# Splitting 512-column products into two of 256, and moving two early transfers, in a two-layer transformer trunk

## The chip, the cores and the metric

The kernel runs on one core of one Trainium2 chip. The metric is the device time of one execution in microseconds (us). The time of the kernel before is the median of three runs. One more execution was profiled, and all rows below come from that one.

## The reference

The reference computes a small decoder trunk on `x` of 256 tokens by 1024 features, all in float32. Layer 0 is differential attention (8 heads, each the difference of two softmaxes over causal scores with a relative-position bias, then an RMS norm per head), a residual with layer norm, and a squared-ReLU MLP of width 4096 with residual and layer norm. Layer 1 has the same shape, with plain 16-head causal attention over a shared K/V in place of the differential one (at 256 tokens there is one block, so the block selection selects nothing).

```python
for layer in range(DEPTH):                       # DEPTH = 2
    mix = diff_attention(h, ...) if layer == 0 else moba_attention(h, ...)
    h = layer_norm(ALPHA * h + mix, ln1_g[layer], ln1_b[layer])
    h = layer_norm(ALPHA * h + square(relu(h @ w_up[layer])) @ w_down[layer],
                   ln2_g[layer], ln2_b[layer])
```

## The kernel before

Every large product is done to nearly float32 precision as three products of operands that are cut in two: a high part and the rest, "hi" and "lo". `three` (L136 to L147) issues hi·hi, hi·lo and lo·hi into one PSUM accumulation. It has two forms. With `moving_w` (L141 to L143) the activations are the stationary operand, 128 tokens wide, and the weights stream past, 512 columns at a time: V, the output projection (`mix`), the first quarter of the MLP's upward product (`up_rows`) and all of its downward product (`down`) are done so. Otherwise (L145 to L147) the weights are stationary and 256 tokens stream past: the Q/K projections (`project`) and the rest of the upward product (`up`). Each product is one weight load and one matmul on TensorE.

All weights stream from memory in units of 128x2048 float32, each in two pieces of 128x1024. `fetch` (L86 to L90) issues the transfer of a piece into one of five `raw` buffers, on SyncE's queue. ScalarE copies the piece to `whi` (L103), VectorE subtracts to get `wlo` (L115), and then the next piece is fetched into the buffer that came free. `bg(n, True)` does `n` such pieces at the place in the program order where it stands; the engines work in that order.

The first two units are special. Eight "chunks" of 128x768 hold, for one block of 128 features each, the transposed input and the first 512 columns of V's weights. `fetch_chunk` puts chunks 0 and 1 into `xres` and chunks 2 to 6 into the five `raw` buffers; chunk 7 is fetched in `v_first`, when chunk 2 has been split (`kk == 2`). When chunks 3 to 7 have been split, `v_first` fetches pieces 4 to 8 (`fetch(kk + 1)`), the first pieces of the units that follow. `V` is a tile of 128x2x1024 that first gets a value after `v_first`, by `v_out`.

Near the end of layer 0's attention the program order is: V's last unit (`v_unit(u0 + 11, 1, 1)`), the exponentials of the last head (`softmax_a(7)`), two pieces, the normalization of that head (`softmax_b(7)`), V's copy out of PSUM (`v_out`), the scaling of the first four heads (`scale`), the transposes of the last head (`turn(7)`) and their copy (`turned(7)`), the transposes of the scaled heads (`o_turn`), and the products with V (`values`). `turn` and `o_turn` take turns in two PSUM banks.

The MLP runs `up` and `down` alternately, so its stages are about 11 us of 256-column products and 11 us of 512-column products in turn. The very last columns of the kernel (the second half of the columns of the second 128 tokens) are already done as products of 256 columns with moving weights.

Of the kernel before, what the change touches and what calls it, by code (L numbers as in the profile page):

```python
# [30 lines left out]
S = 256  # L31
DEPTH = 2
NK = D // P
# [19 lines left out]
def trunk(ctx: ExitStack, tc: tile.TileContext, x, first, units, lam_a, subln, rel_bias,  # L53
          ln_g, ln_b, ident_in, out):
    nc = tc.nc
# [29 lines left out]
    def fetch(q):  # L85

        if q < NU * PER:
            v, s = divmod(q, PER)
            raws[q] = wpool.tile([P, PIECE], F32, name="raw", bufs=RAWS)
            nc.sync.dma_start(raws[q], units[v, s])  # L90
# [30 lines left out]
    def bg(most=8, force=False):  # L121

        while most > 0 and (force or state["credit"] >= 1.0 / PER):
            if not piece():
                state["credit"] = min(state["credit"], 1.0)
                return
            state["credit"] -= 1.0 / PER
            most -= 1
# [8 lines left out]
    def three(ps, w, a, moving_w, n, start, stop):  # L137

        state["credit"] += n * PACE
        if moving_w:  # L140
            nc.tensor.matmul(ps, a[0], w[0], start=start, stop=False)  # L141
            nc.tensor.matmul(ps, a[0], w[1], start=False, stop=False)  # L142
            nc.tensor.matmul(ps, a[1], w[0], start=False, stop=stop)  # L143
        else:
            nc.tensor.matmul(ps, w[0], a[0], start=start, stop=False)  # L145
            nc.tensor.matmul(ps, w[0], a[1], start=False, stop=False)  # L146
            nc.tensor.matmul(ps, w[1], a[0], start=False, stop=stop)  # L147
# [7 lines left out]
    def at(k, h):  # L155
        return act[0][:, k, tokens(h)], act[1][:, k, tokens(h)]

    xres = const.tile([P, 2, D], F32, name="xres")
    chunks = {}

    def fetch_chunk(k):

        if k < 2:
            chunks[k] = xres[:, k, :S + 512]
        else:
            chunks[k] = wpool.tile([P, PIECE], F32, name="raw", bufs=RAWS)[:, :S + 512]
        if k == 0:
            nc.sync.dma_start(chunks[k][:, :S], first[k][:, :S])
            nc.scalar.dma_start(chunks[k][:, S:], first[k][:, S:])
        else:  # L170
            nc.sync.dma_start(chunks[k], first[k])
# [164 lines left out]
    def attention(layer, u0):  # L336
# [4 lines left out]
        with tc.tile_pool(name=f"attn{layer}", bufs=2) as pool, \  # L341
                tc.tile_pool(name=f"attnc{layer}", bufs=1) as one:
            V = one.tile([P, 2, D], F32, name="V")
# [17 lines left out]
            def v_first(u):  # L361

                if u == 0:
                    for h in range(2):
                        pv[0, h] = bank("a")
                split[u] = (wpool.tile([P, 2048], F32R, name="whi", bufs=AHEAD),
                            wpool.tile([P, 2048], F32R, name="wlo", bufs=AHEAD))
                hi, lo = (w.rearrange("p (k c) -> p k c", k=4) for w in split[u])
                for k in range(4):
                    kk = 4 * u + k  # L370
                    split_to(act[0][:, kk], act[1][:, kk], chunks[kk][:, :S])
                    split_to(hi[:, k], lo[:, k], chunks[kk][:, S:])
                    if kk == 2:
                        fetch_chunk(7)
                    elif kk > 2:
                        fetch(kk + 1)
                    if kk == 6:
                        nc.scalar.dma_start(scr, line)
                    a = [at(kk, h) for h in range(2)]
                    for h in range(2):  # L380
                        nc.tensor.matmul(pv[0, h], a[h][0], hi[:, k], start=kk == 0, stop=False)
                    for h in range(2):
                        nc.tensor.matmul(pv[0, h], a[h][1], hi[:, k], start=False, stop=False)
                    for h in range(2):
                        nc.tensor.matmul(pv[0, h], a[h][0], lo[:, k], start=False, stop=kk == NK - 1)
                state["piece"] = state["head"] = (u + 1) * PER
                state["credit"] += PACE
                used.add(u)

            if layer == 0:  # L390
                v_first(0)
                v_first(1)
                free.update(used)
                bg()
                for h in range(2):
                    v_out(0, h)
            else:
                for h in range(2):
                    for c in range(2):
                        pv[c, h] = bank("a")  # L400
                        for g in range(2):
                            u = u0 + 2 * c + g
                            hi, lo = unit(u, k=4)
                            for k in range(4):
                                three(pv[c, h], (hi[:, k], lo[:, k]), at(4 * g + k, h), True, 1 / 8,
                                      g == 0 and k == 0, g == 1 and k == 3)
                                if (h, c, g) == (0, 1, 1) and k % 2 == 0:
                                    ln_turn(1, k // 2)
                            if h == 1:
                                used.add(u)  # L410
                                bg(2, True)
                        v_out(c, h)
# [94 lines left out]
            def turn(p):  # L507
                t, _ = T.pop(p)
                AT[p] = []
                for m in range(1 if diff else 2):  # L510
                    pt = bank("c")
                    for j in range(3):
                        k = (j + 2) % 3
                        nc.tensor.transpose(pt[:, j * P:(j + 1) * P], t[:, m, k * P:(k + 1) * P], ident)  # L514
                    AT[p].append(pt)
# [124 lines left out]
            if diff:  # L640
                turn(5)
                v_unit(u0 + 10, 1, 0)
                halves_hi(7)
                softmax_a(6)
                halves_lo(7)
                turned(5)
                scale = rms(0, [O[0][:, h] for h in range(2)], nc.gpsimd)
                bg(1)
                softmax_b(6)
                scores(7)  # L650
                turn(6)
                v_unit(u0 + 11, 1, 1)
                turned(6)
                softmax_a(7)
                bg(2, True)
                softmax_b(7)
                for h in range(2):
                    v_out(1, h)
                for h in range(2):
                    scale(h)  # L660
                turn(7)
                turned(7)
                o_turn(0, 0)
                o_turn(0, 1)
                bg(2, True)
                for p in range(4, 8):
                    values(p)
                mix(0, 0, G0)
                scale = rms(4, po, nc.vector)
                scale(0)  # L670
                scale(1)
                bg(3, True)
                mix(0, 1, G0)
                mix(1, 0, G0[:2])
                o_turn(4, 0)
                mix(1, 0, G0[2:])
                o_turn(4, 1)
                bg(2, True)
                for c in range(2):
                    mix(0, c, G1)  # L680
                    if c == 0:
                        bg(1, True)
                    ln_add(0, c * 512, c * 512 + 512, pw[0, c])
                ln_apply(layer, 0, 512)
                bg(1, True)
                mix(1, 1, G0)
            else:
                turn(5)
                mix(0, 0, G0[:2])
                values(4)  # L690
                turned(5)
                mix(0, 0, G0[2:])
                halves_hi(7)
                softmax_a(6)
                halves_lo(7)
                softmax_b(6)
                scores(7)
                values(5)
                turn(6)
                mix(0, 1, G0)  # L700
                softmax_a(7)
                turned(6)
                collect(4)
                bg(1, True)
                softmax_b(7)
                bg(1, True)
                values(6)
                mix(1, 0, G0)
                turn(7)
                turned(7)  # L710
                bg(2, True)
                mix(0, 0, G1[:2])
                values(7)
                collect(6)
                mix(0, 1, G1[:2])
                bg(1, True)
                for c in range(2):
                    mix(0, c, G1[2:])
                    ln_add(0, c * 512, c * 512 + 512, pw[0, c])
                ln_apply(layer, 0, 512)  # L720
                mix(1, 1, G0)
# [257 lines left out]
```

## Time and profile before

| | |
|---|---|
| median of 3 runs | 594.53 us (593.96 to 594.57) |
| profiled execution: time | 595.0 us |
| profiled execution: span | 592.9 us |
| TensorE matmuls: busy | 580.7 us, 98% of the span, 3768 matmuls |
| TensorE weight loads: busy | 515.6 us, 87% |
| VectorE, ScalarE busy | 377.7 us (64%), 318.8 us (54%) |
| mean granted TensorE clock | 0.996 of full speed |

The span is what the profiler saw of the engines; the 2.1 us between it and the execution's time lie around it. Matmuls overlap in the profile, since each one's duration runs to the end of its pipeline; what a product costs in a dense stretch is therefore the distance from its start to the next one's start.

### The profile page before, as it was taken

Reading aid. Unit: us, or ns where it says so; the run is one execution under the profiler, and the core shown is the slowest. Engines: PE = TensorE matmul, PEld = TensorE weight load, DVE = VectorE, ACT = ScalarE, POOL = GpSimd, SP = SyncE. Lnnn points to the kernel's source line nnn. Section 1 sums busy time; section 2 is a strip of 40 time slices with the busy share of each in tenths; the row PEclk is TensorE's granted clock in tenths of the full one; section 3 lists DMA queues with packets and bytes.
Section 4 is the critical chain, followed back from the end, with each engine's and each line's share of the span. In section 5 each row is a group of like instructions: output and inputs, shape, how many; then the busy total and the mean of one; then the engine's idle time right before and its main releaser. Section 6 shows DMA issues by size and latency. Waiting matters only on the chain.

```text
span 592.9 us, 9651 instructions
## 1 busy us (share of the span) xinstructions
PE 580.7 (98%) x3768; PEld 515.6 (87%) x3768; DVE 377.7 (64%) x692; ACT 318.8 (54%) x540; POOL 14.2 (2%) x45
## 2 busy tenths in 40 slices
PE   9999999999999999999999999999999999999993
PEld 7899978889899899898889999878899899899883
DVE  5787778976743734553877777697785544554236
ACT  5776787357664654552446556542785564564100
POOL 3000030000000000000000000000000000000000
PEclk9999999999999999999999999999999999999998
DMA  8996755547755737755249745151788556553002
GB/s 274 326 349 212 244 175 170 176 137 271 253 202 213 252 138 249 238 162 205 73 170 331 269 144 166 57 178 36 232 317 294 185 180 213 186 170 107 1 0 71
DMA packets 35548, 113.03 MB, mean 191 GB/s; under 512 B 3872, under 2 KB 8880, under 8 KB 35504
## 3 DMA queue, kind: packets, MB, share of 16 engines
q1 hardware_dynamic: 34144, 107.95, 53.2%
q0 software_dynamic: 1152, 4.19, 2.2%
q8 instruction: 29, 0.48, 0.3%
q10 hardware_dynamic: 208, 0.29, 0.1%
q14 instruction: 15, 0.12, 0.1%
HBM read 111.35 MB, written 1.07 MB: 190 GB/s over the span
## 4 chain that ended last, share of the span: by engine, by line
PE 93%; ACT 2%; DMA 2%; DVE 2%; issue 0%; SPq 0%; DVEq 0%; ACTq 0%
PE ps_b L145 12%; PE ps_b L147 12%; PE ps_b L146 12%; PE ps_a L143 12%; PE ps_a L142 12%; PE ps_a L141 12%; PE ps_b L141 4%; PE ps_b L143 4%; PE ps_b L142 4%; PE ps_a L461 2%; PE ps_c L290 1%; PE ps_c L514 1%; DMA raw<-in_first 1%; DMA raw<-in_units 1%; ACT whi L103 1%; PE ps_a L549 1%
## 5 line engine op out<-in xcount | busy, mean ns | idle before, releaser
L115 DVE TENSOR_TENSOR wlo<-raw,whi 128x1024 fp32r<-128x1024 f32 x188 | 222.2, 1220 | 57.8 <-ACT whi L103 55.8
L103 ACT ACTIVATE whi<-raw 128x1024 fp32r<-128x1024 f32 x188 | 190.1, 1052 | 71.9 <-PE ps_a L143 52.2
L145 PE MATMUL ps_b<-act_hi,whi 128*128 128x256 f32 x640 | 180.0, 281 | 0.0
L147 PE MATMUL ps_b<-act_hi,wlo 128*128 128x256 f32 x640 | 177.8, 278 | 0.8 <-DVE wlo L115 0.8
L146 PE MATMUL ps_b<-act_lo,whi 128*128 128x256 f32 x640 | 177.6, 278 | 0.0
L145 PEld LDWEIGHTS ps_b<-act_hi,whi 128*128 128x128 f32 x640 | 120.2, 188 | 1.7 <-issue 0.7
L147 PEld LDWEIGHTS ps_b<-act_hi,wlo 128*128 128x128 f32 x640 | 120.3, 188 | 1.1 <-DVE wlo L115 1.1
L146 PEld LDWEIGHTS ps_b<-act_lo,whi 128*128 128x128 f32 x640 | 120.7, 189 | 0.5
L143 PE MATMUL ps_a<-whi,h_lo 128*128 128x512 f32 x248 | 97.7, 394 | 0.0
L142 PE MATMUL ps_a<-wlo,h_hi 128*128 128x512 f32 x248 | 97.2, 392 | 0.0
L141 PE MATMUL ps_a<-whi,h_hi 128*128 128x512 f32 x248 | 96.5, 389 | 0.0
L74 DVE TENSOR_TENSOR h_lo<-sqr,h_hi 128x512 fp32r<-128x512 f32 x24 | 16.6, 692 | 77.6 <-ACT h_hi L72 77.6
L142 PEld LDWEIGHTS ps_a<-wlo,h_hi 128*128 128x128 f32 x248 | 46.6, 188 | 10.3
L141 PEld LDWEIGHTS ps_a<-whi,h_hi 128*128 128x128 f32 x248 | 46.6, 188 | 9.9
L143 PEld LDWEIGHTS ps_a<-whi,h_lo 128*128 128x128 f32 x248 | 46.6, 188 | 9.3
L751 ACT ACTIVATE relu<-ps_b 128x512 f32<-128x512 f32 x32 | 19.1, 596 | 65.4 <-PE ps_b L147 54.0
L481 ACT ACTIVATE t<-t,mx 128x256 f32<-128x256 f32 x64 | 28.4, 444 | 31.8 <-DVE mx L478 31.8
L141 PE MATMUL ps_b<-whi,act_hi 128*128 128x512 f32 x96 | 39.1, 407 | 0.0
L143 PE MATMUL ps_b<-whi,act_lo 128*128 128x512 f32 x96 | 37.7, 393 | 0.0
L142 PE MATMUL ps_b<-wlo,act_hi 128*128 128x512 f32 x96 | 37.5, 390 | 0.0
L141 PE MATMUL ps_a<-whi,act_hi 128*128 128x512 f32 x80 | 32.2, 402 | 0.0
L142 PE MATMUL ps_a<-wlo,act_hi 128*128 128x512 f32 x80 | 31.4, 392 | 0.0
(136 smaller groups left out, 587.1 us busy)
## 6 DMA issues: line engine op xcount, KB each, us to landing
raw<-in_units SPq DMA_DIRECT2D x188, 512.0 KB, 4.6
bias<-scr SPq DMA_DIRECT2D x16, 256.0 KB, 5.0
raw<-in_first SPq DMA_DIRECT2D x6, 384.0 KB, 6.1
lnp<-in_ln_g POOLq DMA_DIRECT2D x4, 512.0 KB, 4.3
lnp<-in_ln_b POOLq DMA_DIRECT2D x4, 512.0 KB, 5.4
xres<-in_x SPq DMA_DIRECT2D x1, 1024.0 KB, 5.6
out<-xres SPq DMA_DIRECT2D x2, 256.0 KB, 2.0
out<-xres SPq DMA_DIRECT2D x4, 128.0 KB, 1.9
```

The lines of the kernel that those rows point to most:

```text
L74: nc.vector.tensor_tensor(lo, src, hi.bitcast(F32), op=ALU.subtract)
L103: nc.scalar.activation(split[v][0][:, c], raws[state["head"]], AF.Copy)
L115: nc.vector.tensor_tensor(split[v][1][:, c], raws.pop(state["piece"]), split[v][0][:, c].bitcast(F32), op=ALU.subtract)
L141: nc.tensor.matmul(ps, a[0], w[0], start=start, stop=False)
L142: nc.tensor.matmul(ps, a[0], w[1], start=False, stop=False)
L143: nc.tensor.matmul(ps, a[1], w[0], start=False, stop=stop)
L145: nc.tensor.matmul(ps, w[0], a[0], start=start, stop=False)
L146: nc.tensor.matmul(ps, w[0], a[1], start=False, stop=False)
L147: nc.tensor.matmul(ps, w[1], a[0], start=False, stop=stop)
L461: nc.tensor.matmul(sc[m][:, c:c + n], a[r, q], b[r, :n], start=i == 0, stop=i == 2)
L481: nc.scalar.activation(t[:, m, s], t[:, m, s], AF.Exp, bias=mx[:, m, j:j + 1], accum_out=sm[:, m, j:j + 1])
L751: nc.scalar.activation(r, ps, AF.Relu)
```

## The change

A product of `three` with moving weights is no longer one matmul of 512 columns but two of 256 columns, one after the other, with the same stationary operand; each of the two has a weight load of its own. The first product of an accumulation (the one that opens it) stays whole. Chunk 7 goes into `V`'s own tile; its transfer is issued before `v_first` and not inside it, and the transfers of pieces 4 to 8 are each issued one chunk earlier. Near the end of layer 0's attention one of the two pieces moves from before `softmax_b(7)` to after `scale`, ahead of `turn(7)`.

```diff
         if moving_w:
-            nc.tensor.matmul(ps, a[0], w[0], start=start, stop=False)
-            nc.tensor.matmul(ps, a[0], w[1], start=False, stop=False)
-            nc.tensor.matmul(ps, a[1], w[0], start=False, stop=stop)
+
+            for i, (x, y) in enumerate(((0, 0), (0, 1), (1, 0))):
+                opens = start and i == 0
+                n = ps.shape[-1] if opens else 256
+                for c in range(0, ps.shape[-1], n):
+                    nc.tensor.matmul(ps[:, c:c + n], a[x], w[y][:, c:c + n],
+                                     start=opens, stop=stop and i == 2 and c + n == ps.shape[-1])
...
-    def fetch_chunk(k):
-
-        if k < 2:
+    def fetch_chunk(k, into=None):
+
+        if into is not None:
+            chunks[k] = into
+        elif k < 2:
             chunks[k] = xres[:, k, :S + 512]
...
-                    if kk == 2:
-                        fetch_chunk(7)
-                    elif kk > 2:
-                        fetch(kk + 1)
+                    if 2 <= kk < NK - 1:
+                        fetch(kk + 2)
...
             if layer == 0:
+                fetch_chunk(7, V[:, 0, :S + 512])
                 v_first(0)
                 v_first(1)
...
                 softmax_a(7)
-                bg(2, True)
+                bg(1, True)
                 softmax_b(7)
                 for h in range(2):
                     v_out(1, h)
                 for h in range(2):
                     scale(h)
+                bg(1, True)
                 turn(7)
                 turned(7)
```

## Rows read from the trace of the kernel before

**Rows 1.** The page: busy time by engine, and the chain that ended last.

```profile
PE 580.7 (98%) x3768; PEld 515.6 (87%) x3768; DVE 377.7 (64%) x692; ACT 318.8 (54%) x540; POOL 14.2 (2%) x45
PE 93%; ACT 2%; DMA 2%; DVE 2%; issue 0%; SPq 0%; DVEq 0%; ACTq 0%
```

**Rows 2.** The page's costliest groups: busy us, mean ns of one.

```profile
L146 PE MATMUL ps_b<-act_lo,whi 128*128 128x256 f32 x640 | 177.6, 278 | 0.0
...
L141 PE MATMUL ps_a<-whi,h_hi 128*128 128x512 f32 x248 | 96.5, 389 | 0.0
...
L141 PE MATMUL ps_b<-whi,act_hi 128*128 128x512 f32 x96 | 39.1, 407 | 0.0
...
L141 PE MATMUL ps_a<-whi,act_hi 128*128 128x512 f32 x80 | 32.2, 402 | 0.0
```

**Rows 3.** Timeline of TensorE, a run of 512-column products: start us, us.

```profile
267.21 0.39 PE L141 MATMUL ps_a<-whi,h_hi 128*128 128x512 f32 x1
...
276.82 0.39 PE L141 MATMUL ps_a<-whi,h_hi 128*128 128x512 f32 x1
```

**Rows 4.** Timeline of TensorE, the kernel's last columns, 256 at a time.

```profile
578.63 0.28 PE L141 MATMUL ps_b<-whi,h_hi 128*128 128x256 f32 x1
...
583.39 0.28 PE L141 MATMUL ps_b<-whi,h_hi 128*128 128x256 f32 x1
```

**Rows 5.** Timeline of TensorE, the first `up` stage of layer 0.

```profile
140.15 0.28 PE L145 MATMUL ps_b<-act_hi,whi 128*128 128x256 f32 x1
...
145.45 0.28 PE L145 MATMUL ps_b<-act_hi,whi 128*128 128x256 f32 x1
```

**Rows 6.** One line (L145), stretch 163.2 to 173 us: duration ns min/median/max.

```profile
L145 PE MATMUL ps_b<-act_hi,whi x29: 276/276/276, 163.3 to 172.8; 128*128 128x256 f32 x29
```

**Rows 7.** The same, 318 to 329 us (layer 1's first projections).

```profile
L145 PE MATMUL ps_b<-act_hi,whi x32: 281/281/281, 317.8 to 328.7; 128*128 128x256 f32 x32
```

**Rows 8.** Timeline of the start, all engines: start us, us, idle before and releaser.

```profile
13.32 0.42 ACT L72 ACTIVATE act_hi<-raw 128x256 fp32r<-128x256 f32 x1 [1.47 <-DMA raw<-in_first]
...
15.17 1.06 ACT L103 ACTIVATE whi<-raw 128x1024 fp32r<-128x1024 f32 x1 [0.92 <-DMA raw<-in_units]
...
16.26 1.22 DVE L115 TENSOR_TENSOR wlo<-raw,whi 128x1024 fp32r<-128x1024 f32 x1 [1.28 <-ACT whi L103]
...
16.51 0.28 PE L146 MATMUL ps_b<-act_lo,whi 128*128 128x256 f32 x1
...
17.54 0.39 PE L147 MATMUL ps_b<-act_hi,wlo 128*128 128x256 f32 x1 [0.75 <-DVE wlo L115]
```

**Rows 9.** SyncE's issues of line L171, all: duration ns, first and last start.

```profile
L171 SPq DMA_DIRECT2D raw<-in_first x6: 328/428/442, 1.6 to 8.6; - x6
```

**Rows 10.** Stretches of 1 us: busy by engine, granted clock, DMA share, GB/s.

```profile
10.00:11.00 1.00, 1.00 (x6) 0.80 (x5) 1.00 (x4) 0.98 (x3) 0.00 (x0) 1.00 0.67 218
...
13.00:14.00 1.00, 1.00 (x6) 0.79 (x6) 0.23 (x1) 0.68 (x2) 0.00 (x0) 1.00 0.70 164
```

**Rows 11.** Timeline around the last head of layer 0, all engines.

```profile
83.72 1.99 ACT L103 ACTIVATE whi<-raw 128x1024 fp32r<-128x1024 f32 x2
...
84.79 1.22 DVE L115 TENSOR_TENSOR wlo<-raw,whi 128x1024 fp32r<-128x1024 f32 x1 [1.75 <-ACT whi L103]
...
85.81 1.29 ACT L347 ACTIVATE V<-ps_a 128x512 f32<-128x512 f32 x2
...
86.06 0.40 PE L143 MATMUL ps_a<-whi,act_lo 128*128 128x512 f32 x1
...
87.32 0.52 PE L514 MATMUL ps_c<-ident,t 128*128 128x128 f32 x3 [0.86 <-DVE R L498]
87.87 0.49 ACT L523 ACTIVATE aT<-ps_c 128x384 f32<-128x384 f32 x1 [0.78 <-PE ps_c L514]
87.99 1.23 PE L290 MATMUL ps_c<-ident,o 128*128 128x128 f32 x8 [0.15 <-DVE o L580]
...
89.06 0.39 PE L538 MATMUL ps_a<-V,aT 128*128 128x128 f32 x2
```

## The prediction

> **What bounds the kernel now.** I read the page first: busy shares and the chain that ended last. TensorE's matmuls are busy 98% of the span, and 93% of the chain lies on TensorE [rows 1]; VectorE (64%) and ScalarE (54%) are far from it. So two things count: what TensorE pays for one product in a dense run, and the few places where it stands still. The page's groups give the number of products of each form [rows 2], but not their price: a matmul of 512 columns "lasts" 389 to 407 ns and one of 256 lasts 278, far more than the distance between two starts, because they overlap. The price comes from the timeline, by dividing a long gapless run by its count. The standing still comes from the timeline at the start and around layer 0's last head, which parts 2 and 3 read.
>
> **The price of a product.** In a run of 512-column products, 42 of them (14 triples) take 276.82 - 267.21 = 9.61 us, 228.8 ns each [rows 3]. The kernel's last columns are already done in the form that the change brings to all: moving weights, 256 columns, a weight load for each. There 42 products take 583.39 - 578.63 = 4.76 us, 113.3 ns each [rows 4]; a pair costs 226.7 ns, 2.1 less than one whole product. But 256-column products have a second pace. In the first `up` stage 45 of them take 145.45 - 140.15 = 5.30 us, 117.8 ns each [rows 5]; a pair would cost 235.6, 6.8 more than a whole one. The recorded duration tells the two paces apart: 276 ns where it is quick [rows 4, 6] and 281 where it is slow [rows 7]. Minimum, median and maximum agree over a whole stage (276/276/276 and 281/281/281), so it is not noise around one value: a run falls into one pace and stays there. What decides which I can't read from the trace. The stage of [rows 6] follows 512-column products and is quick; that of [rows 7] follows 512-column products too, and is slow; that of [rows 5] follows transposes. The group of [rows 2] with 256 columns (640 products, 177.6 us, so 277.5 ns each) says how often: (277.5 - 276) / (281 - 276) = 0.3, so some three in ten of today's 256-column products run slow, or a little fewer, since the first of a run is longer in any case.
>
> **Part 1, the split.** Moving weights of 512 columns are used in 248 + 96 + 80 = 424 triples [rows 2], 1,272 products. One opens each accumulation and stays whole: 6 for V, 8 for `mix`, 8 for `up_rows`, 8 for `down`, 30 in all. So 1,242 products become 2,484, with as many loads. All quick: 1,242 x -2.1 ns = -2.6 us. All slow: 1,242 x +6.8 ns = +8.4 us. These are the two ends. I take 95% quick: the only rows that show this very form are quick without exception, and they stand right behind 512-column products, as the split runs of V, `mix`, `up_rows` and the first `down` will stand behind the whole products that open them. That is 1,242 x (0.95 x -2.1 + 0.05 x 6.8) = -2.1 us. It lies on the path, as TensorE is the path, and nothing else changes pace: the credit that `three` gives to the background pieces is counted as before, and VectorE and ScalarE have a third of their time free [rows 1]. That more instructions must be issued costs nothing that I can find: a stage of 256-column products issues at this rate for 10 us without a gap [rows 6].
>
> **A rule against it.** The pair of [rows 4] shows no fixed price for a matmul beside its columns. The Trainium skill, "TensorE: Matmul & The Clock Gate", section "Back-to-back issue gap", gives the gap at full clock as the columns over 2.4 plus 2.5 ns; by that, 1,242 extra matmuls would cost 3.1 us and the sum would end slower. The quick rows disagree with it, the slow ones point its way.
>
> **Part 2, chunk 7 and the first pieces.** TensorE starts layer 0's first projection and stands still for the low part of piece 4: L146 starts at 16.51, L147 at 17.54 [rows 8]. Less one pace of 0.11, 0.92 us are lost. The chain back is short: `wlo` starts at 16.26, as soon as `whi` (15.17) is done, and `whi` waited 0.92 us for the transfer. That piece is asked for only when chunk 3 has been split, and chunk 7, six issues down the line, only at 8.6 us [rows 9], when chunk 2 has been split. The transfers then run dry: the DMA engines' share falls to 0.67 at 10 to 11 us and to 0.70 at 13 to 14 us [rows 10]. With chunk 7 asked for behind chunk 6, without a wait, and each piece one chunk earlier, these holes fill. One chunk is some 1.1 us of VectorE work or more (four subtractions and copies a chunk, VectorE busy all of 10 to 11 us [rows 10]), so piece 4 should land near 14.1, `whi` end at 15.2 and `wlo` at 16.4, just before 16.51. ScalarE is free then: chunk 7, which it took at 13.32 after 1.47 us of waiting [rows 8], comes earlier as well. From there TensorE is dense, so the gain lasts to the end. Bounds: -0.92 (the whole stall) and 0 (the transfers are bound by their rate, and the order alone changes). I take -0.9, since the two holes add up to 0.6 us of all DMA engines and the requests come a whole chunk earlier. `V` is not written until `v_out`, long after chunk 7 has been split, so its loan costs nothing.
>
> **Part 3, the moved piece.** TensorE's last V product starts at 86.06, and `turn(7)` only at 87.32, 0.86 us idle; then the first four transposes of `o_turn` at 87.99, and `values` at 89.06 [rows 11]. VectorE is late because of `wlo` at 84.79 (1.22 us), which waited for its `whi` [rows 11]. With that piece behind `scale`, `softmax_b` can start when the exponentials end near 83.8, and `turn(7)` follows V's products at once. But on ScalarE the second of the two `whi` (1.0 us of the 1.99) now stands between V's copies and `turned(7)`. The copies end at 85.81 + 1.29 = 87.10; `whi` then ends at 88.1, and the copy `aT` runs from 88.1 to 88.6 instead of from 87.87 to 88.36. The second half of `o_turn` needs the bank that `aT` reads, and then takes four transposes of 0.11: `values` start near 89.1, where they start now. TensorE's wait moves from ahead of `turn(7)` to the middle of `o_turn`. I take 0. Bounds: -0.9 if ScalarE doesn't hold it (`turn(7)`, `aT` and `o_turn` all move up by the idle time), +0.3 if `aT` is late by the whole 0.23 and the moved `wlo` then delays `act_lo`.
>
> **Sum.** -2.1 - 0.9 + 0 = -3.0 us. The profiled execution took 595.0, 0.5 above the median of 594.53; taken from the median, the forecast is 591.5.
>
> **Rivals.** *The two paces share as today.* At 0.3 slow, a product changes by 0.7 x -2.1 + 0.3 x 6.8 = +0.6 ns, together +0.7 us; with the start, -0.2: 594.3. For it: the entries into runs keep their kinds. Against it: whole-product runs, which now lie between stages, are gone. *A long stretch falls into the slow pace.* In each layer's MLP, `up` and `down` alternate for over 100 us with nothing between that could change the pace. In one layer 380 split products lose 6.8 + 2.1 ns (3.4 us), and 480 products of `up` that are quick today lose 4.5 ns each (2.2 us): -3.0 + 5.6 = +2.6, so 597.1; with both layers 602.7. It decides the sign when more than 0.32 of the split products are slow (8.9 ns x 0.32 - 2.1 = 0.72 ns, which is the 0.9 us of the start). For it: [rows 5, 7] are slow from end to end. Against: [rows 4]. *Every matmul has a fixed price.* If what [rows 5] show holds for any split (6.8 ns a pair), +8.4 - 0.9 = +7.5: 602.0. The Trainium skill's section named above is this rival's rule, with a smaller figure. *The start doesn't gain*, because the transfers are rate-bound: -2.1, so 592.4.
>
> **Chances and range.** Forecast 0.52; paces as today 0.20; a long slow stretch 0.17; a fixed price 0.05; no gain at the start 0.06. A difference of 0.2%, 1.2 us, is about what can be told from none. Faster than that: the forecast and the start's rival but for their near edge, and a fifth of the "as today" case: 0.60. Same: 0.14, most of the "as today" case. Slower: 0.26. The likeliest case's own range is 590.6 (-0.92 - 2.6 and a little from part 3) to 593.0 (no gain from one of the two terms). For 8 in 10 it must reach up to the case of one slow layer: 590.5 to 597.3.
>
> **What would show it.** Matmuls near 5,010. L141 to L143's successors with 256 columns at 276 ns, two starts 113.3 apart, in most stretches; 281 in a long one would prove the slow rival. No wait of TensorE for `wlo` at 16 to 18 us, chunk 7 copied before 13 us. Around the last head, `turn(7)` right behind V's products, `values` about as long behind V's last product as now (3.0 us). I am wrong if the 256-column stages that aren't touched change their pace, or if the load of a second equal weight costs or saves something that the last columns don't show.

## The result and the profile after

The changed kernel takes 600.75 us (median of 4 runs, 600.47 to 602.16) against 594.25 us for the kernel before (4 runs, 593.88 to 594.57): a ratio of 1.0112, 95% interval 1.0099 to 1.0125. The forecast was 591.5 with a range to 597.3. The kernel is 6.5 us slower, not 3 us faster, and the range doesn't hold the time.

The page of the changed kernel, with the rows that answer to [rows 1, 2]:

```profile
span 599.0 us, 12133 instructions
...
PE 587.8 (98%) x5010; PEld 576.5 (96%) x5010; DVE 378.8 (63%) x692; ACT 319.2 (53%) x540; POOL 14.5 (2%) x45
...
PE 98%; DVE 1%; ACT 0%; DVEq 0%; issue 0%
...
L150 PE MATMUL ps_b<-act_lo,whi 128*128 128x256 f32 x640 | 178.2, 279 | 0.0
```

There are 5,010 matmuls, 3,768 + 1,242 as counted. TensorE is still 98% busy, and the chain now lies on it from end to end: there is less waiting on it (93% of it was TensorE before, 98% is now), and yet it is longer: the products grew dearer. Even the group of L150, 640 products that the change does not touch (L146 in [rows 2]), went from 278 to 279 ns.

The dearer products show one line at a time and one stage at a time. L149 is the first product of `up` (L145 before), L146 is now every product with moving weights. The view of one line, for the four stages behind layer 0's first `down` stage, `up` and `down` in turn; columns are count, minimum/median/maximum duration in ns, first and last start in us, shape:

```profile
L149 PE MATMUL ps_b<-act_hi,whi x29: 281/281/281, 162.8 to 172.7; 128*128 128x256 f32 x29
...
L146 PE MATMUL ps_a<-whi,h_lo x30: 279/279/279, 173.9 to 183.9; 128*128 128x256 f32 x30
...
L149 PE MATMUL ps_b<-act_hi,whi x30: 276/276/276, 185.0 to 194.9; 128*128 128x256 f32 x30
...
L146 PE MATMUL ps_a<-whi,h_lo x30: 276/276/276, 196.0 to 205.7; 128*128 128x256 f32 x30
```

The first row answers to [rows 6]: the same stage, with unchanged code, went from 276 to 281. The stages go slow, slow, quick, quick, and so on: `up` and the `down` behind it share a pace, and at each joint from `down` to the next `up` the pace turns over. This holds through both layers' MLPs. Of these stages only the first `down` of each layer changes pace inside itself. It holds the opening products of four accumulations, whole products that stand singly among split ones. It starts slow, and at the last of the four (154.58) it turns quick and stays so. TensorE's timeline there (x2 is a pair of halves):

```profile
154.34 0.40 PE L146 MATMUL ps_a<-whi,h_lo 128*128 128x256 f32 x2
154.58 0.40 PE L146 MATMUL ps_a<-whi,h_hi 128*128 128x512 f32 x1
154.81 0.39 PE L146 MATMUL ps_a<-wlo,h_hi 128*128 128x256 f32 x2
155.04 0.39 PE L146 MATMUL ps_a<-whi,h_lo 128*128 128x256 f32 x2
```

And the kernel's last columns, the very rows on which the price of a split product rested [rows 4], are slow now, though their code is the same too. One line of them before, and two after:

```profile
L141 PE MATMUL ps_b<-whi,h_hi x14: 276/276/276, 579.0 to 583.4; 128*128 128x256 f32 x14
...
L146 PE MATMUL ps_b<-whi,h_hi x16: 280/280/280, 584.2 to 589.5; 128*128 128x256 f32 x16
L146 PE MATMUL ps_b<-wlo,h_hi x16: 279/279/279, 584.4 to 589.7; 128*128 128x256 f32 x16
```

Neither the clock nor the transfers explain it. The windows of these four stages (busy us and count of TensorE, granted clock, DMA share, GB/s):

```profile
162.80:173.00 10.20, 10.20 (x89) 1.00 0.50 192
173.90:183.90 10.00, 10.00 (x87) 1.00 0.76 233
185.30:195.00 9.70, 9.70 (x88) 1.00 0.29 117
196.00:206.00 10.00, 10.00 (x90) 1.00 0.90 287
```

The granted clock is 1.00 in the slow stages and in the quick ones, and the quick stages hold both the lowest and the highest DMA share.

**Where the time went.** Counted over the whole trace, 1,798 distances between the starts of two split products lie at 116 to 119 ns and 582 at 112 to 115: 76% run slow. Of the distances between untouched 256-column products with stationary weights that lie in one of these two bands, 517 of 1,831 (28%) were slow before and 897 of 1,841 (49%) are now. With the prediction's prices: 1,242 x (0.24 x -2.1 + 0.76 x 6.8) = +5.8 us for the split, 1,920 x 0.21 x 4.5 ns = +1.8 for the untouched products, 48 x 4.5 ns = +0.2 for the last columns, and -0.8 for the two moved transfers (measured alone, below): +7.0, where +6.5 was measured.

At the start and around the last head the trace looks as part 2 and part 3 said. The timeline of the start:

```profile
11.95 0.42 ACT L72 ACTIVATE act_hi<-V 128x256 fp32r<-128x256 f32 x1
...
13.22 1.06 ACT L103 ACTIVATE whi<-raw 128x1024 fp32r<-128x1024 f32 x1 [0.33 <-DMA raw<-in_units]
14.32 1.23 DVE L115 TENSOR_TENSOR wlo<-raw,whi 128x1024 fp32r<-128x1024 f32 x1 [0.70 <-ACT whi L103]
...
16.65 0.28 PE L150 MATMUL ps_b<-act_lo,whi 128*128 128x256 f32 x1
16.77 0.28 PE L151 MATMUL ps_b<-act_hi,wlo 128*128 128x256 f32 x1
```

Chunk 7 is copied at 11.95 (13.32 in [rows 8]), piece 4's `whi` starts at 13.22 (15.17) and its `wlo` at 14.32 (16.26). The third product now follows the second by 0.12 us, where it stood 1.03 behind. The trace of one more kernel (`split_only`, below) qualifies this: it issues chunk 7 and the pieces in the old order, and the stall isn't there either:

```profile
16.03 0.28 PE L150 MATMUL ps_b<-act_lo,whi 128*128 128x256 f32 x1
16.14 0.28 PE L151 MATMUL ps_b<-act_hi,wlo 128*128 128x256 f32 x1
```

So the stall of [rows 8] belongs to some executions of the old order and not to all. In the ten profiled executions with the new order it never shows. The timeline around the last head of layer 0:

```profile
85.02 0.49 PE L519 MATMUL ps_c<-ident,t 128*128 128x128 f32 x3
...
85.71 1.05 ACT L103 ACTIVATE whi<-raw 128x1024 fp32r<-128x1024 f32 x1
...
85.80 0.63 PE L296 MATMUL ps_c<-ident,o 128*128 128x128 f32 x4 [0.29 <-DVE o L585]
...
86.66 0.48 ACT L528 ACTIVATE aT<-ps_c 128x384 f32<-128x384 f32 x1
...
87.19 0.66 PE L296 MATMUL ps_c<-ident,o 128*128 128x128 f32 x4 [0.76 <-ACT aT L528]
...
87.69 0.39 PE L543 MATMUL ps_a<-V,aT 128*128 128x128 f32 x2
```

`turn(7)` starts right behind V's products (at 85.02). The wait of 0.86 us that stood ahead of it [rows 11] is now one of 0.76 in the middle of `o_turn`, for `aT`, which stands behind the moved piece's `whi` on ScalarE.

### The profile page after: what moved, and what is told of

The parts are those of the page before. It is cut to its first block, busy times and chain, and to the rows that moved or that the text cites. A ratio compares the mean times of both kernels' runs of the same rounds, so it can differ in the third digit from the quotient of the medians.

```text
span 599.0 us, 12133 instructions
## 1 busy us (share of the span) xinstructions
PE 587.8 (98%) x5010; PEld 576.5 (96%) x5010; DVE 378.8 (63%) x692; ACT 319.2 (53%) x540; POOL 14.5 (2%) x45
## 4 chain that ended last, share of the span: by engine, by line
PE 98%; DVE 1%; ACT 0%; DVEq 0%; issue 0%
PE ps_a L146 38%; PE ps_b L149 13%; PE ps_b L151 12%; PE ps_b L150 12%; PE ps_b L146 12%; PE ps_a L466 2%; PE ps_c L519 1%; PE ps_c L296 1%; PE ps_a L554 1%; PE ps_a L385 1%; PE ps_a L387 1%; PE ps_c L190 1%; PE ps_a L389 1%; PE ps_c L780 1%; PE ps_a L543 0%; PE ps_a L545 0%
## 5 line engine op out<-in xcount | busy, mean ns | idle before, releaser
L149 PE MATMUL ps_b<-act_hi,whi 128*128 128x256 f32 x640 | 180.5, 282 | 0.0
L150 PE MATMUL ps_b<-act_lo,whi 128*128 128x256 f32 x640 | 178.2, 279 | 0.0
L149 PEld LDWEIGHTS ps_b<-act_hi,whi 128*128 128x128 f32 x640 | 121.0, 189 | 1.0 <-issue 0.7
L150 PEld LDWEIGHTS ps_b<-act_lo,whi 128*128 128x128 f32 x640 | 120.4, 188 | 0.0
L146 PE MATMUL ps_a<-whi,h_hi 128*128 128x256 f32 (+1 forms) x488 | 98.0, 281 | 0.0
L146 PE MATMUL ps_a<-wlo,h_hi 128*128 128x256 f32 x496 | 98.0, 278 | 0.0
L146 PE MATMUL ps_a<-whi,h_lo 128*128 128x256 f32 x496 | 97.7, 278 | 0.0
L146 PEld LDWEIGHTS ps_a<-wlo,h_hi 128*128 128x128 f32 x496 | 75.9, 188 | 0.4
L146 PEld LDWEIGHTS ps_a<-whi,h_lo 128*128 128x128 f32 x496 | 75.4, 188 | 0.0
L146 PEld LDWEIGHTS ps_a<-whi,h_hi 128*128 128x128 f32 x488 | 74.5, 188 | 0.0
L146 PE MATMUL ps_b<-whi,act_hi 128*128 128x256 f32 (+1 forms) x180 | 39.4, 294 | 0.0
L146 PE MATMUL ps_b<-whi,act_lo 128*128 128x256 f32 x192 | 38.1, 279 | 0.0
L146 PE MATMUL ps_b<-wlo,act_hi 128*128 128x256 f32 x192 | 38.1, 279 | 0.0
L146 PE MATMUL ps_a<-whi,act_hi 128*128 128x256 f32 (+1 forms) x150 | 32.7, 293 | 0.0
L146 PE MATMUL ps_a<-wlo,act_hi 128*128 128x256 f32 x160 | 31.8, 279 | 0.0
```

The source lines that it names most:

```text
L146: nc.tensor.matmul(ps[:, c:c + n], a[x], w[y][:, c:c + n], start=opens, stop=stop and i == 2 and c + n == ps.shape[-1])
```

## The experiments

Four theories were in play. **A**: a run of 256-column products has two paces and takes over the pace of the run before it; the whole 512-column products between stages used to set it afresh, and the split took them away. **B**: each split product has a fixed price. **C**: the moved transfers do the harm. **D**: two consecutive loads of the same weights make the slow pace.

**The change taken apart.** The first kernel is the one before with nothing but the split; the second is the changed one without the split:

```diff
-            for i, (x, y) in enumerate(((0, 0), (0, 1), (1, 0))):
...
+            nc.tensor.matmul(ps, a[0], w[0], start=start, stop=False)
+            nc.tensor.matmul(ps, a[0], w[1], start=False, stop=False)
+            nc.tensor.matmul(ps, a[1], w[0], start=False, stop=stop)
```

> Only the split; chunk 7, the first pieces and the moved piece as before. Theory A (two paces, each run inherits one): the 6.5 us of the change plus what the other edits gained until 90 us (1.3 us), so about 602 us, 600 to 604, since other runs at the start may fall into the other pace. Theory B (a fixed price of some 6.8 ns for every split product): 1,242 x 6.8 ns = 8.4 us, 602.7. Theory C (the moved transfers do the harm): no slower than 595.

> Only the other two edits, every product whole. A and B: 593.0 us (-0.9 at the start, -0.2 around the last head, up to 1.5 in all, by the trace of the changed kernel). C: 600 or more.

The split alone: 601.57 us, ratio 1.0117 (1.0100 to 1.0133), with the same turns of pace in the MLP (the time can't tell A from B, which expected 602 and 602.7). The rest alone: 593.62, ratio 0.9984 (0.9974 to 0.9993), 0.84 us less than the 594.46 of the kernel before in the same series. C falls. In the trace of the second kernel V's last unit starts at 72.82 (73.88 before, -1.06) and `mix` at 90.51 (91.66, -1.15), so the stretch between them, with the moved piece, gives 0.1. How much of the rest is the stall isn't shown by these two traces: in the first projection the pace differs as well (mean distance 117.4 ns before, 113.6 here), and in the trace of `split_only`, with the old order, V's last unit starts at 71.67, earlier than in either.

**Split only in `down`, without and with whole products at the joints.** A flag on `three` splits only the products of `down`. In the second kernel the last triple of each `down` stage (three products, the last ones before the next `up`) stays whole; the first has `True` in place of that condition:

```diff
-                n = ps.shape[-1] if opens else 256
+                n = 256 if split and not opens else ps.shape[-1]
...
-                                  first, (c, f) == (end, 3))
+                                  first, (c, f) == (end, 3), not (j == 1 and h == 1 and k == 1 and n == 1))
```

> The changed kernel, but only the products of `down` are split; V, `mix` and `up_rows` are whole. A: the MLP alternates between the paces as in the changed kernel (its two long stretches took 143.1 and 145.0 us against 140.6 and 142.4 before, +5.1), so about 598 us. B: 760 x 6.8 ns = +5.2, also 598, with all 256-column products of `down` slow.

> As down_split, but the last triple of each `down` stage stays whole, 512 columns, as all products ahead of `up` were in the kernel before, where `up` then was quick 10 times of 10. A: all `up` and `down` stages behind it quick, 750 x -2.1 ns = -1.6 and -1.3 for the other edits: 591.4 us. B: 598, as down_split.

Without: 598.36 us, 1.0067 (1.0052 to 1.0082). With: 591.75 us, 0.9959 (0.9946 to 0.9972). 42 whole products are worth 6.6 us, although each of them replaces a pair of halves that could run quicker. A fixed price (B) can't do that: with the pace kept quick, splitting 694 products of `down` takes the time from 593.62 (no split at all) down to 591.75, -1.9 us, where 694 x -2.1 ns is -1.5. The view of one line in the second kernel, for the first stages that were slow in the changed one:

```profile
L149 PE MATMUL ps_b<-act_hi,whi x28: 276/276/276, 162.8 to 172.0; 128*128 128x256 f32 x28
...
L146 PE MATMUL ps_a<-whi,h_hi x27: 276/276/388, 173.7 to 182.6; 128*128 128x256 f32 x26, 128*128 128x512 f32 x1
```

All stages from there to the end of the MLP are quick.

**Whole products at one joint only.** If the pace is inherited, whole products at the first joint alone must not heal the stages, but turn the whole pattern round.

```diff
-                                  first, (c, f) == (end, 3), not (j == 1 and h == 1 and k == 1 and n == 1))
+                                  first, (c, f) == (end, 3), not (c == 0 and j == 1 and h == 1 and k == 1 and n == 1))
```

> As down_split, but only the last triple of the first `down` stage of each layer (c = 0) stays whole. A, with the pace inherited and turned over at each joint from `down` to `up`, as in the changed kernel's trace: the pattern is turned upside down. `up` 3, 5 and 7 and `down` 1, 3 and 5 to 7 become quick, `up` 4 and 6 and `down` 2 and 4 slow; 384 fewer slow products in each layer, 2 x 384 x 4.4 ns = -3.4 us against down_split: 595.0 us. If the whole products act by their number: two triples in 256 change nothing that can be measured, 598.

595.32 us, 1.0014 (1.0005 to 1.0023). The view of one line, the same stages and one more:

```profile
L149 PE MATMUL ps_b<-act_hi,whi x28: 276/276/276, 162.6 to 171.7; 128*128 128x256 f32 x28
...
L146 PE MATMUL ps_a<-wlo,h_hi x28: 276/276/276, 173.7 to 182.6; 128*128 128x256 f32 x28
...
L149 PE MATMUL ps_b<-act_hi,whi x26: 281/281/281, 185.1 to 193.9; 128*128 128x256 f32 x26
...
L146 PE MATMUL ps_a<-wlo,h_hi x28: 279/280/280, 195.9 to 205.2; 128*128 128x256 f32 x28
```

Quick, quick, slow, slow: the changed kernel's pattern inverted, in both layers, through to the last `down` stages. One triple in each layer sets the paces of the hundred microseconds behind it.

**Whole products in the middle of a slow stage.** The 8th of 16 triples of the second `down` stage stays whole, and no other:

```diff
+                                  first, (c, f) == (end, 3), not (c == 1 and j == 0 and h == 1 and k == 1 and n == 1))
```

> As down_split, but the 8th of the 16 triples of the second downward stage (c == 1) of each layer stays whole, in the middle of a stage that ran slow. If a whole 512-column product sets the quick pace wherever it stands, that stage turns quick half way, and all stages behind it are inverted against down_split: up 4 and down 2 slow, up 5 and down 3 quick, up 6 and down 4 slow, up 7 and the last three quick. That is one_reset with up 3 (96 products x 4.4 ns) and half of down 1 (24 pairs x 8.9 ns) slow in each layer, +1.3 on 595.3: 596.6 us. Rival: the whole triple acts only at the joint of two stages: the stage stays slow and the time is that of down_split, 598.4.

596.58 us, 1.0035 (1.0023 to 1.0047), where 596.6 was worked out. TensorE's timeline at that place (x2 is a pair of halves):

```profile
172.19 0.40 PE L146 MATMUL ps_a<-wlo,h_hi 128*128 128x256 f32 x2
...
176.19 0.40 PE L146 MATMUL ps_a<-whi,h_hi 128*128 128x256 f32 x2
176.43 0.40 PE L146 MATMUL ps_a<-wlo,h_hi 128*128 128x256 f32 x2
176.66 0.40 PE L146 MATMUL ps_a<-whi,h_lo 128*128 128x256 f32 x2
176.90 0.40 PE L146 MATMUL ps_a<-whi,h_hi 128*128 128x512 f32 x1
177.13 0.39 PE L146 MATMUL ps_a<-wlo,h_hi 128*128 128x512 f32 x1
177.37 0.39 PE L146 MATMUL ps_a<-whi,h_lo 128*128 128x512 f32 x1
177.60 0.39 PE L146 MATMUL ps_a<-whi,h_hi 128*128 128x256 f32 x2
177.82 0.39 PE L146 MATMUL ps_a<-wlo,h_hi 128*128 128x256 f32 x2
...
182.81 0.39 PE L146 MATMUL ps_a<-whi,h_lo 128*128 128x256 f32 x2
```

Up to the whole triple the pairs stand 0.23 to 0.24 us apart (0.40 long); behind it 0.22 to 0.23 (0.39 long). By the second and last pairs ahead of it and the first and last behind it: (176.66 - 172.19) / 19 = 235 ns and (182.81 - 177.60) / 23 = 226.5. The same code, in the same stage, with the same buffers, changes pace at the whole products.

**How many whole products it takes.** As the kernel with whole triples at every joint, but only the last product of each `down` stage stays whole:

```diff
-                n = 256 if split and not opens else ps.shape[-1]
+                n = 256 if i < int(split) and not opens else ps.shape[-1]
...
-                                  first, (c, f) == (end, 3), True)
+                                  first, (c, f) == (end, 3), 2 if j == 1 and h == 1 and k == 1 and n == 1 else 3)
```

> As down_split_reset, but only the last product of each downward stage is whole, not the last triple. If one whole product is enough to set the pace: every stage quick, 591.7 us. Rival: one is too short (the products before it are still in flight) and the alternation comes back: 598.4.

598.62 us, 1.0073 (1.0059 to 1.0086): as if nothing were whole. The first of its `up` stages behind a `down`, the view of one line:

```profile
L149 PE MATMUL ps_b<-act_hi,whi x28: 281/281/281, 162.7 to 172.3; 128*128 128x256 f32 x28
```

At these joints one whole product does not set the pace, three do: behind a whole triple all 30 `up` stages are quick, but for their first products, in the three kernels that have one at every joint. Neither number is a rule beyond the joints. Inside the first `down` stage a single whole product turned the pace (154.58 in the changed kernel), and three other single ones ahead of it did not. And [rows 7] show a stage right behind some 50 whole products that runs slow from end to end; it does so in `no_split` too, while the same code in `down_split` is quick there:

```profile
L149 PE MATMUL ps_b<-act_hi,whi x32: 276/276/279, 318.9 to 329.5; 128*128 128x256 f32 x32
```

**Everything split, with whole products at the ends.** As the changed kernel, so with V, `mix` and `up_rows` split too, but the first product and the last triple of each accumulation, and the last triple of each `down` stage, whole:

```diff
-                n = ps.shape[-1] if opens else 256
+                n = ps.shape[-1] if opens or stop or whole else 256
...
-                                  first, (c, f) == (end, 3))
+                                  first, (c, f) == (end, 3), j == 1 and h == 1 and k == 1 and n == 1)
```

> As after, with V, mix and the first upward quarter split too, but the first product and the last triple of each accumulation and the last triple of each downward stage whole. About 440 more split products than in down_split_reset. If the whole products at the joints keep these stages quick as well: 440 x -2.1 ns = -0.9, so 590.8 us. Rival: stages that are entered from transposes or from waits fall slow between their whole ends (440 x +6.8 ns = +3.0): 594.7.

594.14 us, 0.9995 (0.9986 to 1.0004); the rival was nearer. Its `up` stages behind `down` are quick, but `up_rows` is mostly slow, as the view of L146 shows:

```profile
L146 PE MATMUL ps_b<-whi,act_lo x57: 276/279/400, 115.5 to 137.7; 128*128 128x256 f32 x54, 128*128 128x512 f32 x3
...
L149 PE MATMUL ps_b<-act_hi,whi x31: 276/276/285, 162.8 to 173.0; 128*128 128x256 f32 x31
```

Against the kernel that splits only `down`, 422 more split products (4,884 matmuls against 4,462) cost 594.14 - 591.75 = 2.4 us, +5.7 ns each, where all slow would be 6.8. Some of that is not theirs: in this kernel's trace the first projection of layer 0 is slow (117.8 ns) and in the other's it is quick (113.5), 0.4 us.

**The order of the halves.** The columns' half is the outer loop and the three products the inner one, so that the two halves of a product no longer stand side by side:

```diff
+            steps = [(i, c, 256) for c in range(0, m, 256) for i in range(3)]
+            if start:
+                steps = [(0, 0, m)] + [t for t in steps if t[0]]
```

> The changed kernel with another order of the six products of a triple: all three of the left half, then all three of the right half, as in the kernel's last columns, so that equal weights no longer follow each other in pairs. A: the pace is inherited whatever the order, and the MLP alternates as before: 599 to 602 us. Theory D (the pairs of equal weights cause the slow pace): quick everywhere, as the last columns were, 590 to 592.

600.79 us, 1.0108 (1.0094 to 1.0122), with the same turns of pace from the first `down` on. This kernel doesn't test D as its expectation says: the first two products of a triple have the same stationary operand, so within each half two equal loads still stand side by side. That is so in the kernel's last columns as well, and they were quick before. D falls by that, by the `down` stage of the changed kernel that has 276 ns (196.0 to 205.7), whose loads come in the same order as those of the one with 279 (173.9 to 183.9), and by the probe's runs of equal weights (below).

**The price of a product by itself.** A kernel that leaves out the whole computation and issues only dense products of several widths, each with its load of weights:

> Leaves out the whole computation and only issues dense products: 48 each of 128, 192, 224, 256, 288, 320, 384, 448 and 512 columns with another weight each time, then 256 columns with weights in equal pairs, 256 and 512 columns with one weight throughout. No time is expected of it; it is for the distance between starts. If a load of about 110 ns binds a product of 256 columns, 128 to 256 columns cost much the same and the price grows from there; if the columns bind it, the price grows in proportion all the way and 256 is half of 512.

TensorE's timeline inside the runs of 128, 224, 256 and 512 columns (start, us from the first start to the last end, count):

```profile
20.79 4.29 PE L29 MATMUL acc<-mv,st 128*128 128x128 f32 x37
...
31.44 4.41 PE L29 MATMUL acc<-mv,st 128*128 128x224 f32 x38
...
36.76 4.84 PE L29 MATMUL acc<-mv,st 128*128 128x256 f32 x39
...
75.24 8.78 PE L29 MATMUL acc<-mv,st 128*128 128x512 f32 x38
```

Less the length of the last one, by the count less one: 111.6 ns at 128 columns, 111.7 at 224, 120 at 256, 226.7 at 512. So up to 224 columns a product with its load has a floor of 111.6 ns, and 512 columns cost 0.443 ns each (288 to 448 columns take 0.451 to 0.461 each, so the price isn't quite in proportion). 256 columns at 0.443 are 113.3, the quick pace; the run of 256 here took 120 instead, and took it again with pairs of equal weights and with one weight throughout. 256 columns is thus the width at which the floor (111.6) and the columns (113.3) nearly meet; that the floor is the load's own price is likely, but no run here times a load alone. The run of equal pairs stands right behind 48 whole products, and yet it and the run behind it, 96 products in all, are slow but for the first two or three:

```profile
L29 PE MATMUL acc<-mv,st x93: 283/283/284, 84.3 to 95.4; 128*128 128x256 f32 x93
```

**The best of it.** As the kernel with whole triples at every `down` joint, with the moved piece behind `turned(7)`, so that its `whi` doesn't hold up `aT`:

```diff
-                bg(1, True)
                 turn(7)
                 turned(7)
+                bg(1, True)
```

> As down_split_reset, but the moved piece stands behind `turned(7)` and not ahead of `turn(7)`. If ScalarE's copy `whi` ahead of `aT` holds the second half of `o_turn`, as part 3 of the prediction says, `values` start 0.75 us earlier: 591.0 us. If not, 591.75 as down_split_reset.

591.63 us (591.40 to 592.11), 0.9953 (0.9941 to 0.9966). TensorE's wait for `aT` is gone and `mix` starts 0.7 us earlier than with the piece ahead of `turn(7)` (89.83 against 90.53), but about 0.4 is left of it some 20 us later, and the time of the whole can't be told from 591.75.

## Why the prediction was wrong

**The price of a product** was read rightly, and the sum by its two paces (227 ns and 236 ns a pair) gives +7.0 against +6.5 measured. B, a fixed price, falls: in the kernels with whole products at the joints the same split saves time.

**Part 1, the step that failed: "I take 95% quick".** Measured, 24% were. Its reason had two halves. The only rows that show this form were quick without exception [rows 4], and it held that the split runs "stand right behind 512-column products", as those do. But [rows 4] stood behind a whole stage of such products, and the split takes that stage away: in the changed kernel the same last columns run at 280 ns. The second half failed by a row that the prediction had read itself: [rows 7] stand right behind 512-column products too, and are slow throughout. What was left, one whole product at the opening of an accumulation, can't be counted on: one whole product at each joint left the time where it was (598.62), and `up_rows`, which has only such openers ahead of most of its split products, ran mostly slow. At one place, in the first `down` stages, such openers did turn the pace to the quick one, at the fourth of them. The evidence for the price was taken from a place whose surroundings the change itself removes.

**"Nothing else changes pace"** failed with it. `up` was quick in the MLP before, behind stages of whole products, and is quick again when only the last triple ahead of it is whole; the slow share of the untouched products rose by 0.21, +1.8 us. The prediction had named this as what would make it wrong, and as the rival of a long slow stretch; its 602.7 for both layers lies 2 us above what was measured. It had the mechanism, at 0.17, and not the form: the slow pace doesn't stay, it turns over at each `down` to `up`, so about half the stages are slow. The argument for 0.17, that nothing lies in the MLP that could change the pace once the whole products are gone, was the stronger one; it weighed less than two rows that couldn't speak for it.

**Part 2** came near in size, in part by luck. It took -0.9 from one execution's stall; the two moves together measured -0.84 by medians, of which some 0.1 is the moved piece. But the old order doesn't always stall, as the trace of `split_only` shows, so the -0.9 was the price of one execution, and how much of the rest is the stall stays open. The rival that only the order of the transfers changes and the start gains nothing doesn't fit the 0.84. **Part 3** was right: the wait moved from `turn(7)` to the middle of `o_turn`, and 0.1 us came of it in the one pair of traces where 0 was taken.

**What stays open.** Why a run keeps its pace, and why the joint from `down` to `up` turns it over while that from `up` to `down` keeps it, isn't settled. At that joint the weights turn from moving to stationary operand; at the other one they turn back. Open too is when whole products set the quick pace: three did at every joint of the MLP and in the middle of a slow stage, one did in the first `down` stages and not at the joints, and some 50 did not ahead of [rows 7]. Shown is that in the MLP the pace is inherited from stage to stage, that a whole triple at a joint or within a stage sets the quick one there, and that the order of the halves, the granted clock and the moved transfers don't decide it.

## What to carry to other kernels

When a price is read from a dense run, read what stands ahead of that run, and ask whether the change takes it away; a minimum, median and maximum that agree over a whole stage are a sign that the pace was decided elsewhere. A product of 256 columns, whose columns take about as long as the floor of a product with its load, was a delicate size here: three longer products at each joint kept it quick and turned a loss of 0.7% into a gain of 0.4%, of which 0.16% comes from the moved transfers. Time the parts of a change one at a time: here 0.8 us of true gain lay under 7 us of loss. And look for a stall in more than one execution before it is priced.

## What the runs showed of the hardware

The same code runs at 113.3 or at 117.8 ns a product for 10 us on end, at a granted clock of 1.00 in both, and the probe found a third value, 120.0. From 128 to 224 columns a product with its load of 128 columns of weights takes 111.6 ns, and a second load of the same weights saves nothing (120.0 ns at 256 columns and 226.7 at 512, as with a new weight each time). The Trainium skill, "TensorE: Matmul & The Clock Gate", section "LDWEIGHTS (loading the stationary operand)", puts a load at its columns over 1.2 in ns; that makes an estimate of 106.7 for 128 columns, near the measured floor. The same page's section "Back-to-back issue gap" says that the spacing of a stream of loads and matmuls is set by both of them (the formula that the prediction took from it is given there for isolated matmuls), which the floor bears out; its sustained figures, some 81 ns at 128 columns and 131 at 512, are not what these runs show (111.6 and 226.7), and the measurements decide.
